# Gated projections interleaved with the last attention head, and cache value tiles taken in ordered pairs, in a two-layer decoder step

## The chip, the cores and the metric

The kernel runs on one core of a Trainium2 chip. The metric is the device time of one launch in microseconds (us). Five engines run their own instruction streams in order: TensorE (PE), VectorE (DVE), ScalarE (ACT), GpSimd (POOL) and SyncE (SP), which here issues the DMAs from one queue. Semaphores order them across engines.

## What is computed

One inference step of a two-layer trunk with width 1024, for 1024 prompt tokens and 64 decode tokens (8 sequences of 8), so T = 1088 columns. Layer 0 is a gated DeltaNet mixer. Layer 1, where the change lies, is a windowed attention with three head groups g of windows 128, 512 and 2048 (dilations 1, 4, 16), eight heads each, and a gate. Its core, cut:

```
proj = einsum('bld,de->ble', h, w_in)
qkv  = proj[..., :3*N_GROUPS*WIDTH_B].reshape(B, L, 3, N_GROUPS, H_B, DH_B)
z    = proj[..., 3*N_GROUPS*WIDTH_B:]
for gi, (window, dil) in enumerate(DIL_GROUPS):
    o, lse = dilated_attn_prompt(q, k, v, window, dil)     # prompt tokens
    o, lse = dilated_attn_step(q, k, v, kv_bufs[gi], ...)  # decode tokens, against the cache
wts = softmax(stack(lses, axis=0), axis=0)
o   = sum(wts[..., None] * stack(outs, axis=0), axis=0)
y   = einsum('ble,ed->bld', o.reshape(B, L, WIDTH_B) * silu(z), w_out)
```

Then follow a gated residual add and a final RMSNorm.

## The kernel before

**Products.** `project` (L122 to L135) makes 128 output columns for all T tokens: three chunks of 384, 384 and 320 tokens, each 8 slices of the contraction times 3 products (high and low parts of inputs and weights: `hh` with `whi`, `hl` with `whi`, `hh` with `wlo`), 72 PE instructions at L130. They accumulate in PSUM tiles `pp`, of which there are two.

**Layer 1's loop** runs over head pairs hp 0 to 3, in each over the groups g = 2, 1, 0, in each over the two heads a = 0, 1. For one (hp, g, a) there are three projections (`proj_tile`: v, k, q; copies at L1105, L1107, L1109), then `attention` with transposes of v and k (L1115), and eight blocks: scores L1151 on PE, mask and minimum L1154 on DVE, exponential L1156 on ACT, transposes L1160 on PE, a copy L1163 or L1165, and the product with the values L1169 on PE. Results go to `stg`; those of g = 2 and g = 1 are stored in DRAM (`gscr`).

**The combine.** After g = 0 of each head, `combine` (L1175 to L1206) weighs the three groups, twice, for four blocks of 128 tokens each ("half"): it loads the other groups' results `stgc` (L1181, two buffers), works out weights on DVE and ACT (L1187 to L1196), scales and adds (ACT L1200, DVE L72), transposes on PE (L1204, four), copies back into an `stgc` buffer (ACT L1205) and stores to `oscr` (L1206). The second half's loads go into the buffer from which the first half's store reads.

**Decode work** is pumped between projections from two queues of generators; `pump(x)` takes x units on average. `qk` holds `decode_scores`: cache key tiles `kc` (L1218, 512 KB), for g = 0 transposed on PE (L1262, four) and multiplied (L1270), for g = 1 and 2 multiplied on DVE with broadcast queries `qb` (L1303); the new tokens' rows at L1242, L1243, L1297, L1298. `pv` holds `decode_out`: per head pair 26 value tiles `vc` of 512 KB (loads L1225, four buffers), each multiplied by 8 small PE instructions at L1345 (two trace records each) into one accumulator; then L1354 sums and L1357 stores. A scheduler puts PE's instructions in one order; the value products of a tile are not tied together.

**After the last head.** The attention of hp 3, a 1, g 0 pumps 1.5 units of `pv` per block, with no projection beside it. Then the attention's pools are closed and new ones opened: eight z heads (`z_phase`, through `gate`: weights, loads `zo` of the attention's output from `oscr` at L397, 72 products, tanh, two DVE steps, and the split into `oh` and `ol`), with three `zo` and three `zt` buffers; then the output projection in two passes, and the normalised rows `yn` (PE L1434, ACT L1436, DVE L1438, store L1440) with three buffers.

## Time and profile before

| | |
|---|---|
| timed runs | 2485.02, 2466.92, 2469.04 us, median 2469.04 |
| profiled execution | 2477.78 us, its span 2476.1 us |
| PE busy | 2335.6 us, 94% |
| DVE busy | 1377.4 us, 56% |
| ACT busy | 926.0 us, 37% |
| POOL busy | 258.0 us, 10% |
| granted TensorE clock, mean over the span | 0.949 |
| read from and written to DRAM | 322.31 MB, 54.27 MB |

Times in the trace are us from the span's start. Layer 1's loop over the first three head pairs lies at about 1180 to 2200, the last head's combine and attention end at 2267.6, the z stage at 2362. A busy time is the sum of an engine's records; PE's records overlap a little, so the distance to the next record's start is the time that one takes up. The granted clock is a share of full speed: 1.0 is TensorE's level of 2.4 GHz, 0.5 that of 1.2 GHz, and values between are means over a stretch.

### The profile page before, as it was taken

To read this page: it belongs to the slowest core of one execution; us is meant where nothing else is said; L and a number is where in the kernel's file an instruction comes from. 1 tells how busy PE (TensorE), PEld (TensorE's weight loads), DVE (VectorE), ACT (ScalarE), POOL (GpSimd) and SP (SyncE) were. 2 spreads that over 40 slices of the span, in tenths; PEclk is the share of its full clock that TensorE was granted. 3 is DMA by queue.
4 is the path that set the end of the run, shared out by engine and by line. 5 is a ranking of instruction groups with operands and counts; after the bars stand their busy time and mean duration, and the time that the engine had idled before them with its cause. 6 is when DMAs were issued, how large, how long until landed. Compare 5 with 4: busy or idle time off the path is not lost.

```text
span 2476.1 us, 43143 instructions
## 1 busy us (share of the span) xinstructions
PE 2335.6 (94%) x16607; PEld 2168.3 (88%) x16607; DVE 1377.4 (56%) x3414; ACT 926.0 (37%) x2453; POOL 258.0 (10%) x399
## 2 busy tenths in 40 slices
PE   7789899989999999899999999999999999998998
PEld 5688788888888898899899999899998999985998
DVE  5678668767875537327743365533655336453434
ACT  5444444444453324233234332343323433232334
POOL 2222222222221202200000000000000000000000
PEclk9989899889899999799999999999999999988999
DMA  9232232232233256339832696626976269657334
GB/s 288 73 84 68 54 96 70 60 83 73 71 79 106 84 157 193 108 88 318 255 91 77 200 328 216 198 77 201 327 215 201 77 199 327 210 181 246 91 108 149
DMA packets 490575, 379.42 MB, mean 153 GB/s; under 512 B 46334, under 2 KB 465391, under 8 KB 490368
## 3 DMA queue, kind: packets, MB, share of 16 engines
q1 hardware_dynamic: 490368, 376.65, 51.6%
q8 instruction: 131, 2.15, 0.4%
q14 instruction: 76, 0.62, 0.1%
HBM read 322.31 MB, written 54.27 MB: 152 GB/s over the span
## 4 chain that ended last, share of the span: by engine, by line
PE 62%; DMA 14%; DVE 13%; issue 5%; ACT 3%; SPq 1%; POOL 1%; POOLq 0%; DVEq 0%; ACTq 0%
PE pp L130 42%; DMA qb<-qscr 3%; DMA DT<-gcscr 2%; PE ps L1151 2%; PE ps L1169 2%; PE sc L1345 2%; DVE ca L72 2%; DVE vtmp L686 2%; DMA wraw<-in_a_w_in_dram 1%; PE ps L1115 1%; DVE pr L1303 1%; DMA vc<-in_cache_kv_w_dram 1%; PE ps L1160 1%; PE ps L151 1%; DVE wlo L115 1%
## 5 line engine op out<-in xcount | busy, mean ns | idle before, releaser
L130 PE MATMUL pp<-hh,whi 128*128 128x384 f32 (+1 forms) x2688 | 913.1, 340 | 13.8 <-DVE cso L552 7.0
L130 PE MATMUL pp<-hl,whi 128*128 128x384 f32 (+1 forms) x2688 | 903.5, 336 | 1.1 <-POOL hl L212 1.1
L130 PE MATMUL pp<-hh,wlo 128*128 128x384 f32 (+1 forms) x2688 | 902.0, 336 | 0.7 <-DVE wlo L115 0.7
L130 PEld LDWEIGHTS pp<-hh,whi 128*128 128x128 f32 x2688 | 513.6, 191 | 31.2 <-issue 10.8
L130 PEld LDWEIGHTS pp<-hl,whi 128*128 128x128 f32 x2688 | 513.5, 191 | 9.2 <-issue 4.1
L130 PEld LDWEIGHTS pp<-hh,wlo 128*128 128x128 f32 x2688 | 511.7, 190 | 5.6 <-issue 2.1
L114 ACT CAST whi<-wraw 128x1024 fp32r<-128x1024 f32 x144 | 150.5, 1045 | 226.0 <-PE pp L130 150.7
L115 DVE TENSOR_TENSOR wlo<-wraw,whi 128x1024 fp32r<-128x1024 f32 x136 | 168.2, 1237 | 95.3 <-ACT whi L114 94.4
L1156 ACT ACTIVATE sm<-sm,stg 128x128 f32<-128x128 f32 (+1 forms) x192 | 86.6, 451 | 344.3 <-DVE stg L1154 312.5
L1303 DVE TENSOR_TENSOR pr<-kc,qb 128x1024 f32<-128x1024 f32 x128 | 154.7, 1218 | 78.9 <-DMA qb<-qscr 50.3
L1293 DVE TENSOR_REDUCE ST<-pr 128x8 f32<-128x1024 f32 x128 | 153.9, 1213 | 1.2
L417 POOL TENSOR_TENSOR ol<-zo,oh 128x384 fp32r<-128x384 f32 x7 | 7.1, 1020 | 1308.9 <-ACT oh L416 1308.9
L72 DVE SCALAR_TENSOR_TENSOR ca<-xin,cwT,ca 128x384 f32<-128x384 f32 (+1 forms) x216 | 133.7, 621 | 9.6 <-ACT ca L556 8.4
L1154 DVE CUSTOM_DVE_ANT_0 sm<-ps,mA 128x256 f32<-128x256 f32 (+1 forms) x128 | 48.4, 378 | 162.1 <-PE ps L1151 150.2
L1169 PE MATMUL ps<-vnat,pT 128*128 128x128 f32 x560 | 98.3, 283 | 5.4 <-DVE pT L1165 5.3
L686 DVE TENSOR_TENSOR vtmp<-Vi,Mi 128x2 f32<-128x2 f32 (+30 forms) x248 | 99.3, 400 | 4.7 <-PE lv L757 0.8
L1151 PE MATMUL ps<-kT,qT 128*128 128x128 f32 (+1 forms) x384 | 95.8, 332 | 5.1 <-DVE stg L1154 5.0
L1169 PEld LDWEIGHTS ps<-vnat,pT 128*128 128x128 f32 x560 | 85.5, 190 | 15.3 <-DVE pT L1165 8.1
L1345 PE MATMUL sc<-vc,Z 128*8 128x128 f32 x1664 | 80.9, 289 | 12.2 <-DMA vc<-in_cache_kv_w_dram 11.5
L1163 ACT COPY pT<-ps 128x256 f32<-128x256 f32 (+1 forms) x96 | 32.4, 338 | 132.7 <-PE ps L1160 129.0
L130 PE MATMUL pp<-oh,whi 128*128 128x384 f32 (+1 forms) x264 | 79.1, 330 | 0.8 <-DVE hh L72 0.8
L1345 PEld LDWEIGHTS sc<-vc,Z 128*8 128x8 f32 x1664 | 41.8, 91 | 39.8 <-DMA vc<-in_cache_kv_w_dram 18.2
(452 smaller groups left out, 3650.2 us busy)
## 6 DMA issues: line engine op xcount, KB each, us to landing
qb<-qscr SPq DMA_DIRECT2D x128, 512.0 KB
vc<-in_cache_kv_w_dram SPq DMA_DIRECT2D x104, 512.0 KB
kc<-in_cache_kv_w_dram SPq DMA_DIRECT2D x104, 512.0 KB
wraw<-in_b_w_in_dram SPq DMA_DIRECT2D x80, 512.0 KB
wraw<-in_a_w_in_dram SPq DMA_DIRECT2D x32, 512.0 KB
aw<-in_ada_w_dram SPq DMA_DIRECT2D x24, 512.0 KB
wraw<-in_ada_w_dram SPq DMA_DIRECT2D x24, 512.0 KB
stgc<-gscr SPq DMA_DIRECT2D x32, 260.0 KB
```

Of the source, the lines that this page charges most:

```text
L72: return (eng or V).scalar_tensor_tensor(out=out, in0=in0, scalar=scalar, in1=in1, op0=op0, op1=op1)
L114: A.copy(out=hi, in_=raw)
L115: (eng or V).tensor_tensor(out=lo, in0=raw, in1=hi.bitcast(F32), op=ALU.subtract)
L130: mm = PE.matmul(acc[:, :cn], lhsT=a[:, k, :], rhs=b[k][:, c0:c0 + cn], start=(n == 0), stop=(n == 3 * KD - 1))
L686: V.tensor_tensor(out=tv, in0=Vi[:, :na, :w], in1=Mi[:, :w, c].unsqueeze(1).broadcast_to([P, na, w]), op=ALU.mult)
L1151: PE.matmul(sv, lhsT=qT[:, b * P:(b + 1) * P], rhs=kT[:, k0:k0 + w], start=True, stop=True)
L1154: V.tensor_tensor_reduce(out=sm[:, :w], in0=sv, in1=mk, scale=1.0, scalar=3e38, op0=ALU.add, op1=ALU.min, accum_out=stg[:, b, 128:129])
L1156: A.activation(out=sm[:, :w], in_=sm[:, :w], func=AF.Exp, scale=-1.0, bias=stg[:, b, 128:129], accum_out=stg[:, b, 129:130])
L1169: PE.matmul(ob[:, (b % 4) * P:(b % 4 + 1) * P], lhsT=pT[:, i * P:(i + 1) * P], rhs=vnat[:, k0 // P + i, :], start=(i == 0), stop=(i == w / ...
L1293: V.tensor_reduce(out=sv[:, n:n + 4, :], in_=pr.rearrange("p (n a e) -> p n a e", a=2, e=P), op=ALU.add, axis=AX.X)
L1303: V.tensor_tensor(out=out, in0=k, in1=q, op=ALU.mult)
L1345: PE.matmul(od[32 * j:32 * j + 8, f * P:(f + 1) * P], lhsT=Z[g][:, a * NB + 2 * j + c, 8 * k:8 * k + 8], rhs=vc[:, j, a * P:(a + 1) * P], ...
```

## The change

Four things change in what runs, and the memory plan makes room for them.

1. `decode_scores` for g = 0 loads both key tiles first, then yields three units, and each key transpose is ordered behind the newest dense product (`newest[0]`).
2. `decode_out` takes value tiles in pairs: a pair is loaded one unit ahead, and all 16 instructions of two tiles are chained in one order, behind the newest product and at high priority. A unit is a pair, so the pumps are halved: 0.9 for 1.8, in the last head 0.5 for 1.5.
3. z head 0 begins after the fourth block of the last attention. The others follow, with 1.8 units of `pv` after each, and the rest of the values at head 6. `oh` and `ol` take slots of tiles that are done by then (`kc`, `qb`, `kT`, `qT`, `vT`, `vc`), which are widened to T columns; `zo` and `zt` are halves of one `KT` slot each: two buffers where there were three.
4. The final stage takes slots by tag too: `yn` has two buffers where it had three.

Tables of layer 0 (`cT`, `SH`, `SC`, `adr`) move into layer 0's pool. The number of PE matrix instructions is the same.

```diff
+    newest = [None]
 
     def project(w, hh, hl, cb, chunks=CHUNKS, each=None):
         whi, wlo = w
@@ -132,6 +130,7 @@
                     if each:
                         each(mm)
                     n += 1
+            newest[0] = mm
...
-        row = wp.tile([P, P], F32, name="adr", bufs=2)
+        row = lc.tile([P, P], F32, name="adr", bufs=2)
...
+    cT = lc.tile([P, KD, 32], F32, name="cT")
+    V.memset(cT, 0.0)
+    SHm = [lc.tile([P, KD, 9], F32, name=f"SH{l}") for l in range(2)]
+    SCm = [lc.tile([P, KD, 9], F32, name=f"SC{l}") for l in range(2)]
...
+    def wide(tag, bufs, name=None, dtype=F32):
+        t = sb.tile([P, T], dtype, name=name or tag, tag=tag, bufs=bufs)
+        return t if name else t[:, :1024]
     def load_cache(g, hp, i):
-        t = sb.tile([P, 4, 256], F32, name="kc", bufs=3)
+        t = wide("kc", 3).rearrange("p (q n) -> p q n", n=256)
...
-        new_rows(g, hp, kf, vf, vnew)
         ST = sb.tile([P, P], F32, name="ST", bufs=1)
         if g == 0:
+            kcs = [load_cache(g, hp, i) for i in range(NT[g])]
+            new_rows(g, hp, kf, vf, vnew)
+            for _ in range(3):
+                yield
             st = sbank()
             for i in range(NT[g]):
-                kc = load_cache(g, hp, i)
+                kc = kcs[i]
                 for a in range(2):
                     tb = sbank()
                     for q in range(4):
-                        PE.transpose(tb[:, q * P:(q + 1) * P], kc[:, q, a * P:(a + 1) * P], ident)
+                        t = PE.transpose(tb[:, q * P:(q + 1) * P], kc[:, q, a * P:(a + 1) * P], ident)
+                        order_after(t, newest[0], "the keys land behind the products before")
...
-                    qb = sb.tile([P, 1024], F32, name="qb", bufs=4)
+                    qb = wide("qb", 4)
...
-        for n, (g, c, k) in enumerate(tiles):
-            vc = load_values(g, hp, c, k)
-            for a in range(2):
-                f = c * 2 + a
-                for j in range(4):
-                    PE.matmul(od[32 * j:32 * j + 8, f * P:(f + 1) * P],
-                              lhsT=Z[g][:, a * NB + 2 * j + c, 8 * k:8 * k + 8], rhs=vc[:, j, a * P:(a + 1) * P],
-                              start=(n == 0 and a == 0), stop=(n == len(tiles) - 1 and a == 1))
+        def load(n0):
+            return [(t, load_values(t[0], hp, *t[1:])) for t in tiles[n0:n0 + 2]]
+        n, nxt = 0, load(0)
+        yield
+        for n0 in range(0, len(tiles), 2):
+            pair, nxt = nxt, load(n0 + 2)
+            prev = newest[0]
+            with tc.high_priority(offset=2000):
+                for (g, c, k), vc in reversed(pair):
+                    for a in range(2):
+                        f = c * 2 + a
+                        for j in range(4):
+                            mm = PE.matmul(od[32 * j:32 * j + 8, f * P:(f + 1) * P],
+                                           lhsT=Z[g][:, a * NB + 2 * j + c, 8 * k:8 * k + 8],
+                                           rhs=vc[:, j, a * P:(a + 1) * P],
+                                           start=(n < 4), stop=(n >= 8 * len(tiles) - 4))
+                            order_after(mm, prev, "one run of products for two value tiles")
+                            prev = mm
+                            n += 1
...
+    oh, ol = [], []
+    class Gated:
+        def __init__(self):
+            self.at = {n: [sb.tile([P, 1024], F32, name=n, tag="KT", bufs=2), 0] for n in ("zo", "zt")}
+        def tile(self, shape, dtype, name, tag, bufs):
+            e = self.at[name]
+            e[1] = 384 - e[1]
+            return e[0][:, e[1]:e[1] + 384]
+    gated = []
+    SLOTS = (("kc", 3), ("kc", 3), ("kc", 3), ("qb", 4), ("qb", 4), ("qb", 4), ("qb", 4), ("kT", 2), ("qT", 2), ("vT", 1),
+             ("kT", 2), ("qT", 2))
+    def z_head(h):
+        if not gated:
+            gated.append(Gated())
+        for i, o in enumerate((oh, ol)):
+            if h < 6:
+                o.append(wide(*SLOTS[2 * h + i], name=f"{'ol' if i else 'oh'}{h}", dtype=F32R))
+            else:
+                o.append(sd.tile([P, T], F32R, name=f"{'ol' if i else 'oh'}{h}", tag="vc", bufs=4))
+        z_phase(gated[0], W1_[:, 9216 + h * P:9216 + (h + 1) * P], h, hh, hl, oh, ol)
...
-                vT = sb.tile([P, NP], F32, name="vT", bufs=1)
-                kT = sb.tile([P, NP], F32, name="kT", bufs=2)
-                qT = sb.tile([P, NP], F32, name="qT", bufs=2)
+                vT = wide("vT", 1)
+                kT = wide("kT", 2)
+                qT = wide("qT", 2)
                 for part, d, ds in ((2, vT, vTs), (1, kT, kTs), (0, qT, qTs)):
                     proj_tile(g, part, h, d, ds)
                     qk.pump(2.2)
-                    pv.pump(1.8)
+                    pv.pump(0.9)
...
-                for _ in attention(g, h, qT, kT, vT, stg):
+                for n, _ in enumerate(attention(g, h, qT, kT, vT, stg)):
                     if last:
-                        pv.pump(1.5)
+                        pv.pump(0.5)
+                        if n == 3:
+                            z_head(0)
...
+    for h in range(1, NH):
+        if h == 6:
+            pv.pump(100.0)
+        z_head(h)
+        pv.pump(1.8)
+    class Last:
+        @staticmethod
+        def tile(shape, dtype, name, bufs):
+            full, tag = {"xr": ([P, 8, 130], "stg"), "sq": ([P, 8, P], "vnat"), "yn": ([P, 4, 130], "stgc")}[name]
+            t = sb.tile(full, dtype, name=name, tag=tag, bufs=2).rearrange("p a b -> p (a b)")
+            return t[:, :shape[1]]
...
+                yn = mp.tile([P, 512], F32, name="yn", bufs=2)
...
     l1.close()
-    zp = ExitStack()
-    zpool = zp.enter_context(tc.tile_pool(name="zp", bufs=1, reuse_waits="tile"))
-    oh, ol = ([zpool.tile([P, T], F32R, name=n, bufs=6) for _ in range(6)] for n in ("oh", "ol"))
-    with tc.tile_pool(name="zt", bufs=1, reuse_waits="tile") as zt:
-        for h in range(NH):
-            if h == 6:
-                pv.pump(100.0)
-                for o in (oh, ol):
-                    o += [sd.tile([P, T], F32R, name=f"oh{i}", tag="vc", bufs=4) for i in range(2)]
-            z_phase(zt, W1_[:, 9216 + h * P:9216 + (h + 1) * P], h, hh, hl, oh, ol)
-            pv.pump(4.0)
...
-                    yn = mp.tile([P, 512], F32, name="yn", bufs=3)
```

The scheduler's order shows what moves on PE. First, PE between the two halves of the combine of the second head pair's first head, before: the last rows ahead of the second half's transpose (line 1204), with the new tokens' rows, two key tiles' transposes from `kc` and their products with `KT`.

```order
L1297 MATMUL lv<-ident,ST 128x128
L1298 MATMUL lv<-kTs,qTs 128x128
L1242 MATMUL lv<-ident,kTs 128x128
L1243 MATMUL lv<-ident,vTs 128x128
L1262 MATMUL lv<-ident,kc 128x128 x4
L1270 MATMUL lv<-qTs,KT 128x8 x4
L1262 MATMUL lv<-ident,kc 128x128 x4
L1204 MATMUL ps<-ident,stg 128x128
```

The same place after, whole, from the first half's four transposes (now line 1207) to the second half's:

```order
L1207 MATMUL ps<-ident,stg 128x128 x4
L128 MATMUL pp<-hh_11264,wlo 128x384
L1310 MATMUL lv<-ident,ST 128x128
L1311 MATMUL lv<-kTs,qTs 128x128
L1250 MATMUL lv<-ident,kTs 128x128
L1251 MATMUL lv<-ident,vTs 128x128
L1172 MATMUL ps<-vnat,pT 128x128 x2
L1207 MATMUL ps<-ident,stg 128x128
```

The key tiles' rows are gone from this place, and of the 20 products that stood ahead of them before only one is left between the two halves.

Second, PE in an attention of the last head pair, before: value tiles (`vc`) between an attention's rows and the products of a projection.

```order
L130 MATMUL pp<-hh_11467,wlo 128x320
L1345 MATMUL sc<-vc,Z_11559 8x128 x8
L1345 MATMUL sc<-vc,Z_11560 8x128
L1169 MATMUL ps<-vnat,pT 128x128
L1151 MATMUL ps<-kT,qT 128x128
L1345 MATMUL sc<-vc,Z_11560 8x128
L1160 MATMUL ps<-ident,sm 128x128
L1345 MATMUL sc<-vc,Z_11560 8x128 x6
L130 MATMUL pp<-hh_10928,whi 128x384
```

After, a value row in such a place (the line is now 1365, a product 128):

```order
L128 MATMUL pp<-hh_11467,wlo 128x320
L1365 MATMUL sc<-vc,Z_11561 8x128 x16
L1163 MATMUL ps<-ident,sm 128x128
L1154 MATMUL ps<-kT,qT 128x256
L128 MATMUL pp<-hh_10928,whi 128x384
```

Before, one tile's eight instructions stand in pieces with attention rows between; after, two tiles' sixteen stand in one row.

Third, PE at the end of the last attention, before: the rows from the last head's first half to the first z products.

```order
L1204 MATMUL ps<-ident,stg 128x128 x4
L1345 MATMUL sc<-vc,Z_11560 8x128 x8
L1169 MATMUL ps<-vnat,pT 128x128 x2
L1345 MATMUL sc<-vc,Z_11560 8x128 x8
L1345 MATMUL sc<-vc,Z_11561 8x128 x72
L1204 MATMUL ps<-ident,stg 128x128 x2
L1345 MATMUL sc<-vc,Z_11561 8x128 x8
L1204 MATMUL ps<-ident,stg 128x128 x2
L1345 MATMUL sc<-vc,Z_11561 8x128 x32
L130 MATMUL pp<-hh_11286,whi 128x320
L130 MATMUL pp<-hl_11287,whi 128x320
```

After, from the third of the last four transposes to the value pairs behind them:

```order
L1207 MATMUL ps<-ident,stg 128x128
L128 MATMUL pp<-hl_11417,whi 128x320
L128 MATMUL pp<-hh_11416,wlo 128x320
L128 MATMUL pp<-hh_11441,whi 128x320
L128 MATMUL pp<-hl_11442,whi 128x320
L128 MATMUL pp<-hh_11441,wlo 128x320
L1207 MATMUL ps<-ident,stg 128x128
L128 MATMUL pp<-hh_11467,whi 128x320
L128 MATMUL pp<-hl_11468,whi 128x320
L128 MATMUL pp<-hh_11467,wlo 128x320
L1365 MATMUL sc<-vc,Z_11560 8x128 x32
L128 MATMUL pp<-hh_10928,whi 128x384
```

Before, no product stands beside the last values, and the z products begin behind them; after, z products stand between the transposes of the last half, and two value pairs behind them (the others stand among later z products).

## Rows read from the trace of the kernel before

**Rows 1.** The page: busy us, share and instructions of each engine; costliest groups, lines left out.

```profile
PE 2335.6 (94%) x16607; PEld 2168.3 (88%) x16607; DVE 1377.4 (56%) x3414; ACT 926.0 (37%) x2453; POOL 258.0 (10%) x399
...
L1345 PE MATMUL sc<-vc,Z 128*8 128x128 f32 x1664 | 80.9, 289 | 12.2 <-DMA vc<-in_cache_kv_w_dram 11.5
```

**Rows 2.** Windows: start:end us, busy PE, PEld, DVE, ACT, POOL (records), clock, DMA share, GB/s.

```profile
2205.90:2226.00 20.10, 17.92 (x80) 16.23 (x79) 7.83 (x36) 8.60 (x25) 0.00 (x0) 0.58 0.21 53
2226.00:2240.70 14.70, 13.31 (x199) 9.82 (x199) 7.30 (x38) 7.62 (x27) 0.00 (x0) 1.00 0.78 243
2240.70:2267.60 26.90, 15.84 (x252) 7.20 (x248) 4.67 (x21) 3.55 (x10) 0.00 (x0) 0.66 1.06 340
2267.60:2362.00 94.40, 94.40 (x595) 93.02 (x592) 41.73 (x71) 31.90 (x58) 8.16 (x8) 0.99 0.31 88
```

**Rows 3.** Timeline, PE, tail: start us, busy us, engine, line, operation, count [idle before <-releaser].

```profile
2228.18 1.06 PE L1345 MATMUL sc<-vc,Z 128*8 128x128 f32 x32
2229.17 0.49 PE L1333 MATMUL lv<-pTn,vnew 128*128 128x128 f32 x2
...
2266.64 1.04 PE L1345 MATMUL sc<-vc,Z 128*8 128x128 f32 x16 [2.29 <-DMA vc<-in_cache_kv_w_dram]
2267.62 0.64 PE L130 MATMUL pp<-hh,whi 128*128 128x320 f32 x1
```

**Rows 4.** Timeline, PE, one value tile in an attention of the second head pair.

```profile
1570.50 0.39 PE L1345 MATMUL sc<-vc,Z 128*8 128x128 f32 x4
1570.83 0.71 PE L1169 MATMUL ps<-vnat,pT 128*128 128x128 f32 x4
1571.47 0.40 PE L1345 MATMUL sc<-vc,Z 128*8 128x128 f32 x6
...
1573.12 0.38 PE L1345 MATMUL sc<-vc,Z 128*8 128x128 f32 x2
1573.43 0.44 PE L130 MATMUL pp<-hh,whi 128*128 128x384 f32 x1
1573.71 0.34 PE L130 MATMUL pp<-hl,whi 128*128 128x384 f32 x1
```

**Rows 5.** Timeline, all engines, combine of the second head pair's first head.

```profile
1579.23 0.60 PE L1204 MATMUL ps<-ident,stg 128*128 128x128 f32 x4
...
1579.67 0.75 PE L1354 MATMUL lv<-comb,odS 128*128 128x32 f32 x6
...
1580.48 0.37 SPq L1206 DMA_DIRECT2D oscr<-stgc  x1
...
1582.85 0.37 SPq L1181 DMA_DIRECT2D stgc<-gscr  x1
...
1585.76 0.17 DVE L1187 TENSOR_TENSOR cm<-cm,stgc 128x4 f32<-128x4 f32 x1 [5.01 <-DMA stgc<-gscr]
...
1590.03 0.33 PE L1204 MATMUL ps<-ident,stg 128*128 128x128 f32 x1 [0.31 <-DVE stg L72]
...
1590.20 1.78 PE L1115 MATMUL ps<-ident,vT 128*128 128x128 f32 x8
...
1592.01 0.81 DVE L1109 COPY vT<-pp 128x384 f32<-128x384 f32 x1 [0.72 <-PE ps L1115]
```

**Rows 6.** Windows at the second head pair's two combines, columns as in rows 2.

```profile
1579.20:1597.40 18.20, 15.36 (x92) 14.64 (x91) 7.50 (x29) 5.70 (x14) 0.00 (x0) 0.81 0.35 98
1635.20:1648.70 13.50, 11.23 (x74) 10.93 (x72) 5.07 (x22) 4.99 (x13) 0.00 (x0) 0.87 0.28 85
```

**Rows 7.** Timeline, all engines, the end of the program.

```profile
2470.62 0.69 ACT L1436 ACTIVATE yn<-ps,rn 128x512 f32<-128x512 f32 x1 [2.15 <-DMA out_y_p_dram<-yn]
```

**Rows 8.** Groups by line, PE, 1180 to 2200: busy us, mean ns, idle before, releasers.

```profile
L1345 PE MATMUL sc<-vc,Z 128*8 128x128 f32 x1248 | 59.9, 273 | 0.0
...
L1270 PE MATMUL lv<-qTs,KT 128*128 128x8 f32 x96 | 13.6, 267 | 6.7 <-ACT KT L1265 4.1 <-DVE cm L1194 1.7 <-ACT stg L1200 0.9
...
L1262 PE MATMUL lv<-ident,kc 128*128 128x128 f32 x48 | 8.9, 308 | 4.9 <-DVE nmd L1299 4.9
```

More of the change, by code (lines that the diff above doesn't have):

```diff
@@ L94 @@
     fgv = vecs[:, 65:73]
-    cT = const.tile([P, KD, 32], F32, name="cT")
-    V.memset(cT, 0.0)
     fold = const.tile([P, 9], F32, name="fold")
@@ L100 @@
         V.tensor_tensor(out=fold, in0=fold, in1=ident[:, i:i + 9], op=ALU.add)
-    SHm = [const.tile([P, KD, 9], F32, name=f"SH{l}") for l in range(2)]
-    SCm = [const.tile([P, KD, 9], F32, name=f"SC{l}") for l in range(2)]
     GTm = [const.tile([P, KD, 9], F32, name=f"GT{l}") for l in range(2)]
@@ L1273, in decode_scores @@
         else:
+            new_rows(g, hp, kf, vf, vnew)
             tb = sbank()
@@ L1441 @@
-    zp.close()
+    for h in range(1, NH):
[9 more added lines that the diff above has]
+            return t[:, :shape[1]]
+    x2 = [Columns("hh", F32) for _ in range(KD)]
@@ new lines, with post2 @@
+    mp = Last
+    for chunks, c0, c1 in ((PASSES[0], 0, WIDE // P), (PASSES[1], WIDE // P, NC + 1)):
+        cs = slice(chunks[0][0], sum(chunks[-1]))
+        def post2(j):
+            A.activation(out=x2[j][:, cs], in_=x2[j][:, cs], func=AF.Copy, scale=fgv[:, j:j + 1])
+        qs = out_project(mp, 1, I["b_w_out"][0], x1scr, x2, oh, ol, post2, chunks)
+        rn = col_stats(qs, c0, c1)
+        for c in range(c0, c1):
+            m = rows(c)
+            for half in range(2):
+                yn = mp.tile([P, 512], F32, name="yn", bufs=2)
+                tb = bank()
+                for q in range(4):
+                    PE.transpose(tb[:m, q * P:(q + 1) * P], x2[half * 4 + q][:, tok(c)], ident)
+                if half:
+                    A.activation(out=yn[:m], in_=tb[:m, :], func=AF.Copy, scale=rn[:m, c:c + 1])
+                else:
+                    V.tensor_scalar(out=yn[:m], in0=tb[:m, :], scalar1=rn[:m, c:c + 1], scalar2=None, op0=ALU.mult)
+                dst = O["y_p"][0, tok(c), :] if c < NC else O["y_s"].rearrange("b l d -> (b l) d")
+                SY.dma_start(out=dst[:, half * 512:(half + 1) * 512], in_=yn[:m])
```

20 lines of the change are left out of this document (removed).

## The prediction

> **What bounds the kernel now.** I read the page's busy shares first: TensorE (PE) is busy for 94% of the span [rows 1], so only time in which PE is idle, slowed or issuing inefficiently can be won. Next the windows by stage, which set PE's busy time beside the granted clock. The z stage is dense at 0.99 [rows 2]; the 61.7 us ahead of it, 2205.9 to 2267.6, are not: 17.92 busy of 20.1 at a clock of 0.58, 13.31 of 14.7 at 1.00, 15.84 of 26.9 at 0.66 [rows 2]. This is the tail, with the last head's combine, its attention and the 26 value tiles of the last head pair, and no dense product to put beside them. In its last third DMA is full (1.06, 340 GB/s) and PE waits for value tiles, 11.5 us in the whole run by the page's group [rows 1]; the last tile comes after 2.29 us of idling, and the z products start right behind it [rows 3]. Third, PE's rows inside attention, where one value tile is cut in pieces [rows 4]. Fourth, all engines at a combine, a chain over five queues [rows 5].
>
> The profiled execution took 2477.78 us (span 2476.1), 0.35% over the median of 2469.04. I work the difference out of the profile and take it off the median.
>
> **1. Tail: gain 17 (6 to 28).** How much of the 61.7 us is content? Upper bound: busy time times clock, 17.92x0.58 + 13.31 + 15.84x0.66 = 34.2. Lower: 26 tiles at 0.495 (two tiles took 0.99, from 2228.18 to the next row at 2229.17 [rows 3]) make 12.9; the windows hold 80 + 199 + 252 records, less 26x16 for the tiles leaves 115, by no less than 0.11 (four L1204 take 0.44 to the next row [rows 5]): 12.7, together 25.6. So content is 26 to 34 and the loss 28 to 36; I take the middle, 32. In the new order z products stand between the attention's blocks and value pairs among later z products, so the loss can be filled. I leave 15:
> - 6.5 for the combine of the last pair's first head, which stays ahead of any z product: its chain needs 12.8 us (part 3), the order puts 6.9 beside it, and the clock falls behind the gap as it does now.
> - 4.5 (0 to 7) for value pairs. A pair is 1.05 MB, 3.1 us at 340 GB/s [rows 2], and I add 2.9 for landing, as a 260 KB load takes from issue to reader [rows 5]: 6.0. Four buffers hold two pairs; where the pump takes two in a row, the order has some 35 products between them, 5.6 us at the z stage's 0.16 a record (595 in 94.4 us [rows 2]). I let 0.5 us stick out at each of the last nine pairs.
> - 3 for the end of z: the last value tile's sums (L1354) and the output stores now stand some 41 products (7 us) ahead of the output projection, and zo has two halves where it had three buffers.
> - 1 for switches.
> The bounds are the loss's lower end with 22 left (pairs waiting throughout), 6, and 36 less 8, 28.
>
> On the pairs' loads the Trainium skill says otherwise ("DMA: Bandwidth & Descriptors", section on the anatomy of one DMA): about 2.0 us fixed plus bytes over 436 GB/s; by this a pair would land in 4.4 us, an estimate, the 4.5 above would be nothing and the tail's gain 21.5. The trace reached 340 GB/s here. Nothing below uses the page's figure.
>
> **2. Whole value tiles: gain 10 (5 to 15).** Before, one tile stands in four pieces of 4, 6, 4 and 2 records (the second of 4 is not shown), 0.38 to 0.40 busy each and 0.31 to 0.33 to the next row (1570.50 to 1570.83, 1573.12 to 1573.43) [rows 4]: 1.3 us against 0.495 whole. Over the first three head pairs the line is busy for 59.9 us in 1248 records [rows 8]; 39 whole pairs would be 39x1.06 = 41.3. A record's end overlaps the next by 0.06 a run, and the order has 32 runs a head pair before, 13 after: 59.9 - 96x0.07 = 53.2 elapsed against 39x0.99 = 38.6, so 15 is saved. But the products themselves are cut into 395 runs where there were 368; a switch costs about 0.19 (the first product behind another line is busy for 0.44 where the next is for 0.34 [rows 4], and the first instruction behind the products holds about as much more): -5. Fifteen if the switches hide, five if the pairs find their loads late.
>
> **3. Combine at the six g = 0 transitions of the first three head pairs: loss 8 (16 lost to 2 gained).** Both halves share buffers, so the second runs behind the first: the L1204 transposes at 1579.23, the store at 1580.48, the load's issue at 1582.85 (2.4 later), the first reader at 1585.76 (2.9 later), the second half's L1204 at 1590.03, 10.8 us after the first. Behind it, and behind eight value transposes (1.78), the copy L1109 at 1592.01 frees the bank that the next projection needs: 12.8 us from the L1204 [rows 5]. PE's time without content is 12.8 less the work that stands between. Before, the order puts 7.0 to 7.8 there at all six: 5.4 each, 32 in all; the windows of two of them lose 18.2 - 15.36x0.81 = 5.8 and 13.5 - 11.23x0.87 = 3.7 [rows 6], so 32 is on the high side by up to 4. After, the cache keys are moved away and I count, row by row at such prices, between the two L1207: 7.5, 3.7, 1.4, 9.9, 1.4, 9.9 (the order of the second head pair shows a 1.4). Where the wait is short (three places) the eight value transposes can stand in it, 1.8 less, and with 0.2 to 0.7 for the half clock behind the long ones: 3.5 + 9.3 + 12.1 + 1.1 + 12.1 + 1.1 = 39. So -8. Not worse than -16: that doubles it. Up to +2: before, PE also waited at these places for the new rows' maximum and the key copies, 4.9 + 6.7 = 11.6 us [rows 8]; if it was these that set the pace, they disappear, since the key transposes now lie among products, and pay for most of the longer gap.
>
> **4. Output buffers: loss 3 (0 to 5).** The normalised rows have two buffers where they had three. At the end a copy already waits 2.15 us for an output store [rows 7]; with two buffers the last six pieces wait once more, +2, and the first pass about once, +1. Nothing if the reciprocal before them is later than the buffers.
>
> **5. The rest: 0 (3 either way).** Tables in the first layer's pool and wider slots change no instruction. The first four value loads move behind other loads on SP's queue at the layers' boundary; those are spaced by their own two buffers.
>
> **Sum**: 17 + 10 - 8 - 3 = 16: 2461.8 for the profiled execution, 2453 against the median.
>
> **The rivals.**
> - *Bare combines cost nothing and the loads are in time (faster).* Part 3 at +2, 8 left in the tail (gain 24), and 10 - 3: 33, 2436. For it: PE's named releasers at the transitions are maxima and key copies, not the combine alone [rows 8]. Against: the chain in [rows 5] is fixed and longer than what the new order puts beside it.
> - *Value pairs starve the z stage (slower).* SP issues pair loads, z's weights and the zo loads from one queue; a pair's load waits there for its buffers, and a zo load behind it is late, or the other way round, and PE stands at a pair because the order places it. Price: a fully exposed pair is 6.0 us; eight in the z stage are 48, less the 4.5 counted: 16 - 43.5 = -27.5, 2496. It decides when the mean wait per pair passes (16 + 4.5)/8 = 2.6 us. For it: DMA at 1.06 in the tail and a pair wait of 2.29 for one tile. Against: z leaves 0.69 of DMA free [rows 2], and two units lie on average between a load and its products.
> - *The filling doesn't happen.* PE runs in order, so where a block of the last attention is late, the z products behind it are late too: tail gain 0, the rest 10 - 8 - 3 = -1, 2470. Against: the z products stand in front of the late instructions in most places of the new order.
>
> **How the numbers follow.** My forecast 0.47 (own range 2441 to 2465), fast rival 0.33 (2425 to 2445), starved z 0.10 (2475 to 2500), no filling 0.10 (2465 to 2475). A measurement of this kernel can tell about 1% from no change, 2444.3 and 2493.7. Faster: nine tenths of the fast rival and a fifth of mine, 0.39. Slower: half of the starved case and a little for a layout cost that I don't see, 0.08. Same 0.53. The range reaches from the fast rival's far end, 2425, to 2480, and leaves out most of the starved case and some of parts 2 and 3 at their ends together.
>
> **What would show it.** Right: PE dense at clock 0.95 or more from the last attention to the output projection, with the stretch from 2205.9 to the z stage's end some 17 shorter; the value line's busy time over the first three pairs falling from 59.9 to about 41; and gaps of 9 to 12 us with a clock under 0.8 at the first-head combines of the second and third head pair. Wrong: value waits of over 2.6 us per pair in z, a low clock in the last attention, or short gaps at those combines.

## The result and the profile after

The changed kernel took 2448.71 us in the median of four runs (2437.65 to 2461.96) against 2475.33 (2466.92 to 2485.02): a ratio of 0.9887, with a 95% interval of 0.9848 to 0.9926. A second timing gave 0.9903 (0.9874 to 0.9933). The prediction was 2453, with a range of 2425 to 2480. The medians of the kernel before lie between 2469 and 2486 from one session to the next, so below a run is compared by its ratio to the before of its own session, or with runs of the same session.

Its profiled execution has a span of 2446.5 us, 29.6 less than before, at a mean clock of 0.951 (0.949 before). The page, engines and the first groups of products; the columns are those of rows 1:

```profile
PE 2294.7 (94%) x16607; PEld 2164.4 (88%) x16607; DVE 1378.7 (56%) x3414; ACT 929.2 (38%) x2453; POOL 256.7 (10%) x399
```

PE has 41 us less busy time [rows 1] with as many instructions; the other engines are as they were.

To find where the time went, I take the start of the same dense product in both traces, counting PE's rows that write `pp` from `hh`, `hl`, `oh` or `ol`. The second timing left a second trace of the changed kernel, which stands beside the first:

| product | what stands there | before | after | second trace after | after - before, both traces |
|---|---|---|---|---|---|
| no. 2376 | end of layer 0 | 978.2 | 977.2 | 976.9 | -1.0, -1.3 |
| no. 7344 | last one ahead of the last head's projections | 2141.8 | 2132.3 | 2138.7 | -9.5, -3.1 |
| no. 7560 | last of that head's projections | 2190.8 | 2177.9 | 2184.4 | -12.9, -6.4 |
| no. 8208 | early in the output projection | 2371.4 | 2339.6 | 2346.7 | -31.8, -24.7 |
| no. 8712 | its end | 2461.9 | 2430.6 | 2437.6 | -31.3, -24.3 |
| | end of the span | 2476.1 | 2446.5 | 2453.5 | -29.6, -22.6 |

The stretch from no. 7344 to no. 8208, the last head and z, is 22 us shorter in both traces; 3.4 of it fall in the head's projections, 18 to 19 behind them. The loop ahead of it gains 8.5 us in the first trace and 1.8 in the second, so its share is known only to some 7 us. Behind no. 8208 about 2 us are given back. The windows of the tail, which answer to [rows 2], with the same columns:

```profile
2191.90:2205.90 14.00, 11.21 (x75) 10.57 (x74) 5.43 (x23) 5.95 (x15) 0.00 (x0) 0.80 0.32 100
2205.90:2226.00 20.10, 20.10 (x154) 19.50 (x154) 11.46 (x43) 11.82 (x31) 1.06 (x1) 0.97 0.65 184
2226.00:2245.20 19.20, 19.20 (x154) 18.42 (x153) 10.07 (x31) 9.66 (x30) 1.53 (x2) 1.00 0.42 127
2245.20:2262.00 16.80, 16.80 (x164) 16.17 (x165) 8.61 (x28) 6.58 (x16) 0.47 (x1) 1.00 0.73 223
2262.00:2340.00 78.00, 73.93 (x690) 70.49 (x684) 27.09 (x44) 22.14 (x39) 5.07 (x5) 0.98 0.60 187
```

From 2205.9 to 2262 PE is dense at a clock of 0.97 to 1.00, where it had gaps in all three windows and a clock of 0.58, 1.00 and 0.66 [rows 2]. What is left is the last pair's first combine (14.0 - 11.21x0.80 = 5.0) and 4 us of idling up to the output projection. PE's waits from 1180 on (sum, times, longest) name that idling, one wait for values and one ahead of the output projection:

```profile
PE pp L128 <- DVE zt L72: 2.7, 1, 2.7
...
PE sc L1365 <- DMA vc<-in_cache_kv_w_dram: 1.4, 1, 1.4
```

The groups by line on PE from 1180 to 2190, which answer to [rows 8]; columns as there. The first line is the combine's transposes before, from 1180 to 2200, the others are after:

```profile
L1204 PE MATMUL ps<-ident,stg 128*128 128x128 f32 x50 | 11.5, 332 | 3.8 <-DVE stg L72 3.8
...
L1365 PE MATMUL sc<-vc,Z 128*8 128x128 f32 x1216 | 40.1, 273 | 0.0
...
L1282 PE MATMUL lv<-qTs,KT 128*128 128x8 f32 x96 | 11.7, 242 | 0.0
L1207 PE MATMUL ps<-ident,stg 128*128 128x128 f32 x48 | 10.9, 338 | 31.6 <-DVE stg L72 29.3 <-ACT knew L1253 2.3
L1273 PE MATMUL lv<-ident,kc 128*128 128x128 f32 x52 | 8.5, 277 | 0.0
```

The value line is busy for 40.1 us in 1216 records (59.9 in 1248 before), the key rows wait for nothing (11.6 before), and the combine's transposes, L1207, now have 31.6 us of idling ahead of them, where L1204 had 3.8. That is the new wait. All engines but PE's products at the second pair's first combine, to hold against [rows 5]:

```profile
1575.55 0.17 DVE L1189 TENSOR_TENSOR cm<-stg,stgc 128x4 f32<-128x4 f32 x1 [0.67 <-DMA stgc<-gscr]
...
1578.91 0.60 PE L1207 MATMUL ps<-ident,stg 128*128 128x128 f32 x4
...
1579.55 0.59 ACT L1208 COPY stgc<-ps 128x512 f32<-128x512 f32 x1
...
1580.16 0.37 SPq L1209 DMA_DIRECT2D oscr<-stgc  x1
...
1582.70 0.37 SPq L1184 DMA_DIRECT2D stgc<-gscr  x1
...
1585.63 0.17 DVE L1190 TENSOR_TENSOR cm<-cm,stgc 128x4 f32<-128x4 f32 x1 [5.13 <-DMA stgc<-gscr]
...
1589.06 0.45 PE L1207 MATMUL ps<-ident,stg 128*128 128x128 f32 x1 [8.37 <-DVE stg L72]
```

The second half starts on its first load at 1575.55, ahead of the first half's transposes; what it waits for is its second load, which is issued only at 1582.70, behind the store of 1580.16 from that same buffer. That it is the store's landing, and not other work in SP's queue, that releases such loads shows in SP's waits from 1180 to 2200 (sum, times, longest); this one ends at 1582.64:

```profile
SPq L1184 <- DMA oscr<-stgc: 16.7, 9, 4.1
```

PE stands for 8.37 us in one piece.

### The profile page after: what moved, and what is told of

Its sections match the earlier page's. It is cut to its first block, busy times and chain, and to the rows that moved or that the text cites. A ratio compares the mean times of both kernels' runs of the same rounds, so it can differ in the third digit from the quotient of the medians.

```text
span 2446.5 us, 43164 instructions
## 1 busy us (share of the span) xinstructions
PE 2294.7 (94%) x16607; PEld 2164.4 (88%) x16607; DVE 1378.7 (56%) x3414; ACT 929.2 (38%) x2453; POOL 256.7 (10%) x399
## 4 chain that ended last, share of the span: by engine, by line
PE 67%; DMA 13%; DVE 10%; issue 6%; ACT 2%; POOL 1%; SPq 1%; POOLq 0%; ACTq 0%; DVEq 0%
PE pp L128 46%; DMA DT<-gcscr 2%; PE ps L1154 2%; PE ps L1172 2%; DMA qb<-qscr 2%; PE sc L1365 2%; PE ps L1118 1%; DMA aw<-in_ada_w_dram 1%; DVE ca L72 1%; DVE vtmp L689 1%; DMA wraw<-in_a_w_in_dram 1%; PE ps L1163 1%; DVE pr L1316 1%; DMA out_kv_s_dram<-knew 1%; PE ps L150 1%
## 5 line engine op out<-in xcount | busy, mean ns | idle before, releaser
L72 DVE SCALAR_TENSOR_TENSOR ca<-xin,cwT,ca 128x384 f32<-128x384 f32 (+1 forms) x216 | 137.3, 638 | 9.6 <-ACT ca L559 8.4
L72 DVE SCALAR_TENSOR_TENSOR hh<-pp,GT,xr 128x384 f32<-128x384 f32 (+1 forms) x48 | 27.3, 571 | 85.0 <-PE pp L128 83.6
L128 PE MATMUL pp<-oh,whi 128*128 128x384 f32 (+1 forms) x216 | 72.0, 333 | 2.7 <-DVE zt L72 2.7
L1157 DVE CUSTOM_DVE_ANT_0 sm<-ps,mG 128x128 f32<-128x128 f32 x64 | 18.4, 288 | 96.5 <-PE ps L1154 67.1
```

What stands on the lines that cost most here:

```text
L72: return (eng or V).scalar_tensor_tensor(out=out, in0=in0, scalar=scalar, in1=in1, op0=op0, op1=op1)
L128: mm = PE.matmul(acc[:, :cn], lhsT=a[:, k, :], rhs=b[k][:, c0:c0 + cn], start=(n == 0), stop=(n == 3 * KD - 1))
L1157: V.tensor_tensor_reduce(out=sm[:, :w], in0=sv, in1=mk, scale=1.0, scalar=3e38, op0=ALU.add, op1=ALU.min, accum_out=stg[:, b, 128:129])
```

## The experiments

Ratios are to the kernel before in the same session.

| run | edit, on which kernel | ratio | 95% interval |
|---|---|---|---|
| changed kernel, first, again | | 0.9887, 0.9903 | 0.9848 to 0.9926, 0.9874 to 0.9933 |
| e1_z_behind | changed: z head 0 written behind the attention | 0.9889 | 0.9868 to 0.9909 |
| e1b_z_held | and its products held behind the last combine | 0.9969 | 0.9950 to 0.9987 |
| e2_tiles_single | changed: value tiles single | 0.9918 | 0.9897 to 0.9938 |
| e3_keys_early | changed: keys where they were before | 0.9857 | 0.9836 to 0.9878 |
| e4_late_half | changed: second half of combine later | 0.9815 | 0.9785 to 0.9845 |
| e5_store_stg | changed: the half stored from another tile | 0.9734 | 0.9706 to 0.9763 |
| e6_both | e4 and e5 | 0.9694 | 0.9667 to 0.9721 |
| e7_before_store | before, with e5's edit alone | 0.9846 | 0.9820 to 0.9872 |
| e8_both_keys | e6 with the keys where they were before | 0.9760 | 0.9736 to 0.9784 |
| e9_both_yn3 | e6 with a third output buffer | 0.9714 | 0.9692 to 0.9737 |

**z behind, and z held.** First only the place in the code is undone:

```diff
-                        if n == 3:
-                            z_head(0)
-    for h in range(1, NH):
+    for h in range(NH):
```

> The changed kernel (ratio to before 0.9887, span 2446.5) with z head 0 written behind the last attention instead of behind its fourth block; slots, value pairs and everything else as in the changed kernel. Theory A (where the z head is written makes the z products available): the last attention has no product beside it again, and 20 to 30 us come back: ratio 0.996 to 1.001. Theory B (what keeps z back in the kernel before is that its tiles need the space of the closed attention pools; with slots by tag the scheduler takes z products forward on its own): no change, ratio 0.985 to 0.992, and z products between the last combine's halves as in the changed kernel.

It made no difference: 0.9889. The scheduler takes z products forward by itself, and 74 of them still stand between the last combine's halves in its order; the same stretch is dense here too:

```profile
2195.00:2262.00 67.00, 63.98 (x569) 61.28 (x570) 31.54 (x104) 31.42 (x82) 3.11 (x3) 0.95 0.60 177
```

So the place in the code is not what makes z products available, and theory A falls. Theory B's other half, that in the kernel before z is kept back by the closed pools, is supported by that kernel's own trace, which shows more than the section on the change says: 48 of the 72 products of z head 0 run there from 2194.0 on, ahead of the last attention. They fill the two `pp` tiles, and the copies out of these into `zt`, a tile of the new pools, come only behind the last transposes. Before, then after:

```profile
2194.00 0.44 PE L130 MATMUL pp<-hh,whi 128*128 128x384 f32 x1
...
2261.20 0.88 ACT L408 ACTIVATE zt<-pp 128x384 f32<-128x384 f32 x2
```

```profile
2203.84 0.88 ACT L411 ACTIVATE zt<-pp 128x384 f32<-128x384 f32 x2
```

No run puts the pools back under the changed kernel, so the slots are the likeliest cause and not a tested one. Then the products themselves are held back:

```diff
+            lastT[0] = PE.transpose(tb[...], X[0][:, n, 0:P], ident)      # in combine
-        z_phase(gated[0], W1_[...], h, hh, hl, oh, ol)
+        gate(gated[0], W1_[...], h, hh, hl, z_split(h, oh, ol),
+             each=(lambda mm: order_after(mm, lastT[0], "...")) if h == 0 else None)
```

> As e1_z_behind, and z head 0's products are ordered behind the last transposes of the last combine, so that no z product stands in the last attention; 26 value tiles still in pairs, most of them among z products. Theory A (the tail's 22 us in the profile come from z products beside the last attention): 15 to 30 us over the changed kernel, ratio 0.994 to 1.000, with clock about 0.6 and idle PE between the last head's transposes. Rival C (they come from value tiles that no longer wait at the end, since their loads spread over the z stage): at most 8 us over the changed kernel, ratio up to 0.992.

It fell to 0.9969, about 20 us over the changed kernel. From product 7344 to 8208 its trace takes 230.9 us, the changed kernel's 207.3, that of before 229.6. Its windows over the last attention show PE with gaps and at a low clock, as before:

```profile
2196.00:2206.00 10.00, 7.72 (x87) 5.72 (x85) 3.40 (x14) 2.02 (x7) 0.00 (x0) 0.71 0.95 288
2206.00:2226.00 20.00, 15.75 (x91) 13.59 (x87) 7.42 (x36) 11.42 (x33) 0.00 (x0) 0.72 0.55 157
2226.00:2262.00 36.00, 24.30 (x118) 20.29 (x119) 12.80 (x60) 12.06 (x35) 0.00 (x0) 0.81 0.24 67
```

All value pairs of the last head pair lie among z products here, and it helps nothing: rival C falls. (In the changed kernel three pairs of 13 still stand in the attention, so the run moves those too.) The changed kernel's gain in the tail is that of products beside the attention.

**Single value tiles.** The code of before for the values, with pumps of 1.8, 1.0 and 3.6:

```diff
-            pair, nxt = nxt, load(n0 + 2)      # and the chained order at high priority
+            vc = load_values(g, hp, c, k)      # one tile, eight products, no order
-                    pv.pump(0.9)
+                    pv.pump(1.8)
```

> The changed kernel with value tiles one at a time, not tied together, loaded in their own unit, and the pumps doubled (1.8, 1.0 and 3.6); all else as changed. The order then has 117 runs of value rows for 47. Theory A (whole tiles gain 10 to 19 us: 15 from the rows' prices over the first three pairs and up to 4 in the last): 8 to 20 us over the changed kernel, ratio 0.991 to 0.997, the value line's busy time over the first three head pairs back near 60 from 41. Rival D (the pairs' pace is what leaves the combines bare, and the shorter rows are given back there): in this order 6.6 and 4.4 us stand in the second and third head pair's combines for 1.0 and 9.1, so the bare gaps shorten by 6 to 8 us and the net is 0 to 8 us over the changed kernel, ratio 0.987 to 0.991.

The ratio of 0.9918 is 0.15 to 0.31 points over the changed kernel's two, 4 to 8 us, between the two theories. The intervals overlap; but e1_z_behind, which times like the changed kernel, took 2453.5 to 2458.7 us in the same session and this kernel 2460.1 to 2472.4, so the sign stands. Its lines on PE tell why (1180 to 2200):

```profile
L1358 PE MATMUL sc<-vc,Z 128*8 128x128 f32 x1168 | 56.6, 273 | 0.0
L1207 PE MATMUL ps<-ident,stg 128*128 128x128 f32 x48 | 11.7, 348 | 18.3 <-DVE stg L72 15.8 <-ACT knew L1253 2.4
...
L1367 PE MATMUL lv<-comb,odS 128*128 128x32 f32 x16 | 3.8, 404 | 8.4 <-ACT odS L1363 8.4
```

The value rows cost about what they did before (56.6 busy in 1168 records), and the combines' transposes wait for 18.3 us in place of 31.6. Not all of the difference is gained: the 8.4 us ahead of the value sums (L1367), which are new, stand in the same combines, 4.2 each at 1597.8 and 1908.6. From the first half's transposes to the second half's, PE idles for 26.6 us over the six combines ahead of the last pair, for 31.7 in the changed kernel. So the pairs' pace lays the combines bare by some 5 us, whole tiles gain more than that, and both theories are half right.

**Keys early.**

```diff
-            kcs = [load_cache(g, hp, i) for i in range(NT[g])]
-            for _ in range(3):
-                yield
-                        order_after(t, newest[0], "...")
+                kc = load_cache(g, hp, i)
```

> The changed kernel with the g = 0 key tiles loaded, transposed and multiplied as in the kernel before (no three units of delay, no order behind products). Theory A (the moved keys took the cover from the combines): the six gaps shrink by 8 to 12 us in sum and the time falls by that, ratio 0.984 to 0.986. Rival D (it is not the keys but the pairs' pace; the order still has 1.1 us in the first combines of the second and third head pair): only the first pair's second combine gains (8.6 for 3.2 us, about 5 us), and waits of the keys' own (some 10 us of maximum and key copy in the kernel before) come back: ratio 0.987 to 0.993.

0.9857, some 7 to 11 us better than the changed kernel by the ratios, with intervals that overlap; against e1_z_behind in the same session (2453.5 to 2458.7) every one of its times, 2442.9 to 2453.0, is lower. The idling ahead of the transposes falls to 17.6 us and little of the key waits returns (1.9 + 1.2 + 1.3):

```profile
L1278 PE MATMUL lv<-qTs,KT 128*128 128x8 f32 x96 | 12.2, 251 | 3.2 <-DVE KT L1275 1.9 <-ACT KT L1273 1.2
...
L1207 PE MATMUL ps<-ident,stg 128*128 128x128 f32 x48 | 10.3, 315 | 17.6 <-DVE stg L72 17.0 <-ACT knew L1253 0.5
L1270 PE MATMUL lv<-ident,kc 128*128 128x128 f32 x52 | 8.3, 279 | 1.3 <-DVE nmd L1307 1.3
```

So the moved keys uncover part of the combines as well. Between the halves of the six combines PE idles for 21.8 us here: of the 31.7, the keys' old place takes away 10, single tiles 5, and neither covers them.

**The combine itself.** The next two attack the round trip from two sides: put it beside products, or shorten it. Later:

```diff
-                    for half in range(2):
-                        combine(h, stg, half)
+                    if hp == 3:
+                        combine(h, stg, 0); combine(h, stg, 1)
+                    else:   # due counts heads; taken behind the k projection of that head
+                        if a:
+                            late.append((6 * hp + 6, h, stg, 0, False))
+                        else:
+                            combine(h, stg, 0)
+                        late.append((6 * hp + 6 + a, h, stg, 1, True))   # True: ordered behind newest[0]
```

> The changed kernel with the second half of the six combines of the first three head pairs written two projections later, its transposes ordered behind the products written before it (35 to 45 us of work now stand between the halves' transposes for 1.0 to 9.1); loads, buffers and arithmetic as they were. Theory A (the combine's round trip lies bare in the changed kernel and costs what PE waits there, 29.3 us before the second transposes, with the low clock behind some 40): 25 to 40 us under the changed kernel, ratio 0.972 to 0.979, and the wait of the transposes on the weighted sum gone. Rival E (PE would wait in these places anyway, for the copies of the projections that free its banks, 6.4 us now, and for the next attention): 0 to 10 us under, ratio 0.985 to 0.989, with the banks' wait grown to 15 us or more.

0.9815, 18 to 22 us under the changed kernel, less than theory A asked. The edit also writes the first half of a pair's second head later. From the first half's transposes to the second half's, the trace has 38 to 48 us in the first three pairs, nearly all of it work; yet 12.7 us of the wait remain (PE's waits from 1180, longest last):

```profile
PE ps L1207 <- DVE stg L72: 12.7, 3, 5.8
PE pp L128 <- DVE vT L1112: 6.8, 4, 2.3
```

They are at 1338.5, 1641.3 and 1940.1, at the first half of the pair's second head: the delayed second half of one head is now followed closely by the first half of the next, and those two share the buffers. The wait moved to the neighbour in the buffers' ring. Rival E isn't right either: the banks' wait stays at 6.8.

The other side needs two lines:

```diff
-        A.copy(out=X[1][:, :, 0:P], in_=v3(tb))
-        SY.dma_start(out=oscr[h]..., in_=X[1][:, :, 0:P])
+        A.copy(out=X[0][:, :, 0:P], in_=v3(tb))
+        SY.dma_start(out=oscr[h]..., in_=X[0][:, :, 0:P])
```

> The changed kernel, but the transposed half goes back into the attention's own result tile and is stored from there, so that the second half's loads need not wait for the store: the round trip of 9.9 us from the first transposes to the second loses the copy, the store and its landing, 3.5 to 3.9 us; nothing is reordered. Theory A (the round trip is what PE waits for): the five bare gaps of 2.3 to 8.5 us shrink by up to 3.7 each, 12 to 18 us under the changed kernel, ratio 0.981 to 0.984. Rival E: 0 to 6 us, ratio 0.986 to 0.989.

0.9734: 38 to 42 us under the changed kernel by the ratios (the two medians of its session differ by 40), more than twice what I expected. All engines but the products, second pair's first combine, in this kernel:

```profile
1569.65 0.37 SPq L1184 DMA_DIRECT2D stgc<-gscr  x1
...
1574.58 0.17 DVE L1190 TENSOR_TENSOR cm<-cm,stgc 128x4 f32<-128x4 f32 x1 [0.59 <-DMA stgc<-gscr]
...
1577.03 0.60 PE L1207 MATMUL ps<-ident,stg 128*128 128x128 f32 x4
...
1578.28 0.36 SPq L1209 DMA_DIRECT2D oscr<-stg  x1
...
1580.95 0.30 PE L1207 MATMUL ps<-ident,stg 128*128 128x128 f32 x1 [2.15 <-DVE stg L72]
```

From the first transposes to the second it takes 3.9 us instead of 10.15. My estimate took away the copy, the store and its landing only. But once the store doesn't hold the buffer, the load is issued at 1569.65, seven microseconds ahead of the first half's transposes, so the load and the second half's weights leave the chain too; what remains is the scaling L72 behind the last block of attention. DVE also no longer stands for 5 us at L1190 with the next blocks' work behind it. Over the six combines ahead of the last pair the times from the first transposes to the second fall from 67.5 to 41.9 us in sum. In the traces, 26.4 us are gained from product 2376 to 7344 and 3.2 more up to 8208, 29.6 against the first trace of the changed kernel; against the second, in which this stretch is 7.4 us longer, it is 37.0. The timing's 38 to 42 lies a little above the second; single executions of one kernel differ by as much.

> e4_late_half and e5_store_stg together. Theory A: once the halves are apart, the shorter round trip is hidden in the first three pairs and only the last pair's first combine gains: ratio 0 to 0.002 below e4_late_half's. Rival E: as e4_late_half. If the two add fully (12 us below e4 or more), the cover of e4 isn't where the time went.

0.9694: 2407.66 us where the changed kernel took 2458.63 and before 2483.67 in that session. That is 29.5 us under e4_late_half's 2437.16, so theory A and rival E both fail and the third case holds: what e4_late_half put beside the combines was not where most of the time went. Against e5_store_stg's 2418.65 the later halves add 11 us. The transposes' idling is gone:

```profile
L1207 PE MATMUL ps<-ident,stg 128*128 128x128 f32 x56 | 8.6, 273 | 0.0
```

From product 2376 to 7344 it is 37.4 us shorter than the changed kernel's first trace and 44.1 shorter than its second; I take that as what the combines cost there.

**The same two lines in the kernel before.**

> The kernel before with e5_store_stg's edit alone (the half is stored from the attention's result tile, so the second half's loads don't wait for the store). Theory A (in the kernel before, too, the round trip outlasts the 7.0 to 7.8 us of work beside it, about 32 us over six combines; the edit takes some 6 us off each trip, as it did in the changed kernel, 10.1 to 3.9 in the second pair's first combine): 15 to 30 us under before, ratio 0.988 to 0.994. Rival F (before, PE's waits there are those for the new rows' maximum and the key copies, which stay): 0 to 8 us under, ratio 0.997 to 1.000.

0.9846, 38 us, more than either theory, and more than the whole change under study gained. From product 2376 to 7344 it gains 20.7 us, the round trips that the prediction had put at 32; from 7344 to 8208 another 18.6, in the tail, which I had not thought of. From 7560 to 8208 it takes 161.1 us, as the changed kernel does (161.7, before 180.6), and with no z product beside the last attention: 48 stand ahead of it, as in the kernel before, and the next one starts at 2229.9, behind it. So products beside the attention are one way to the tail's gain and not the only one; in the kernel before, the combines' stores held the attention up as well. The windows of the second pair's combines, against [rows 6]:

```profile
1584.20:1594.00 9.80, 9.75 (x71) 9.49 (x70) 6.80 (x26) 4.95 (x13) 0.00 (x0) 1.00 0.55 156
1633.80:1645.00 11.20, 11.20 (x87) 11.13 (x86) 4.75 (x12) 4.99 (x11) 0.00 (x0) 1.00 0.21 46
```

Dense at full clock, with the keys where they were. Of PE's 11.6 us of waits for maxima and key copies [rows 8] 0.5 are left, in the tail. That fits engines DVE and ACT that stood at the combine's load with this work behind them in their queues; it is read from the waits, not tried by itself. Rival F falls.

**Keys and output buffers, on e6.**

> e6_both with the g = 0 keys loaded, transposed and multiplied as in the kernel before. Theory A (the keys' move pays where it doesn't uncover the combine: the waits for the maximum and the key copies, 11.6 us in the kernel before, are what it removes): with the combines covered the old place costs 4 to 12 us, ratio 0.971 to 0.974. Rival G (the keys' place is indifferent by itself): ratio 0.968 to 0.971 as e6_both (0.9694).

0.9760 against 0.9694 and 0.9714 of kernels with the moved keys: 0.5 to 0.7 points, 11 to 16 us, over the upper end of theory A; rival G falls. By the medians of its own session it is 9.4 us over e9_both_yn3, of which some 2 belong to that kernel's third output buffer, and from product 2376 to 7344 the traces have 6 to 8 us (1124.0 against 1117.7 in e6_both and 1116.4 in e9_both_yn3). So the direction stands and the size is some 6 to 16 us. With the combines bare, in e3_keys_early, the sign is the other one.

> e6_both with a third buffer for the normalised output rows, taken from the slot of the natural keys. Theory A (two buffers cost 2 to 3 us at the end): the last 20 us of the trace are 2 us shorter; ratio 0.968 to 0.969, which the timing can't tell from e6_both's 0.9694; the trace decides.

0.9714, and in the same session as e8. The time can't tell it from e6. In the traces the last six pieces of the output run from 2398.85 to 2405.28 in e6, with four waits for a store's landing, and from 2396.70 to 2400.96 here, with two: 2.2 us less. The last piece in each:

```profile
2405.28 0.68 ACT L1504 ACTIVATE yn<-ps,rn 64x512 f32<-64x512 f32 x1 [2.19 <-DMA out_y_p_dram<-yn]
```

```profile
2400.96 0.68 ACT L1511 ACTIVATE yn<-ps,rn 64x512 f32<-64x512 f32 x1 [0.74 <-DMA out_y_p_dram<-yn]
```

## Why the prediction came out right, and where it didn't

The sign and the range came out as forecast. The size is less clear a hit than 2449 against 2453 looks, because the median of before had moved by 6 us in between: by the ratios, 0.9887 and 0.9903 of the 2469.04 that the prediction started from are 2441 to 2445, the lower end of my own range and the upper end of the fast rival's. 24 to 27 us of gain lie between my forecast's 16 and the rival's 33. What tells the two apart is the mechanism: the rival needed bare combines that cost nothing, and PE idles for 31.6 us at them. The terms:

1. **Tail, 17 (6 to 28): 18 to 19**, from no. 7560 on, in both traces; the last head's projections, which the term left out, give 3.4 more. That the products do it is shown by e1b_z_held: without them that stretch takes 185.9 us (before 180.6, changed kernel 161.7). By e7_before_store it is not the only way. What is left was less than I had set aside in two places: 5.0 at the combine instead of 6.5, and one wait of 1.4 for values instead of 4.5. At the end of z there are 2.69 us of idling and 3.4 us at a granted clock of 0.5 behind them. The step on the pairs' loads had 5.6 us between a load and its products; in the trace the last nine pairs have 6.3 to 23 us from the second tile's load to the first product. By the fit that the Trainium skill gives ("DMA: Bandwidth & Descriptors", the anatomy of one DMA) this part would have been nothing; that section gives it for loads issued by way of GpSimd, and these go through SP. The one pair that PE waited for, issued at 2291.3 and 2291.8 behind another pair, was read at 2299.45, 7.7 us behind the second issue, which is longer than the fit's 4.4 and than my 6.0; no row shows how long a pair's transfer takes by itself.
2. **Whole tiles, 10 (5 to 15): more, some 16.** The value line's busy time fell as worked out (41 forecast; 40.1 in 1216 of 1248 records). Measured to the next row, a tile takes 0.50 us where it took 0.68 on average before: 14 us over 78 tiles, for the 15 worked out. The 5 us against it, for more runs of products, were too many: to the next row, the 4968 products from no. 2376 to 7344 take 870.2 us for 868.0 (871.9 in the second trace). And a term was missing: the attention's rows, no longer cut by value rows, take 148.7 us there for 154.7 (155.5 with single tiles, in e2_tiles_single).
3. **Combines, -8 (-16 to 2): worse, at or past the lower bound.** The count from the order was right: less PE's idling, the times from the first half's transposes to the second half's are 7.9, 4.0, 1.8, 10.2, 1.8 and 10.2 us, for 7.5, 3.7, 1.4, 9.9, 1.4 and 9.9. The gaps at the first heads of the second and third pair are 8.4 and 8.6 us long, at clocks of 0.77 and 0.69, for the 9 to 12 that were to show it. The step that failed is the price of a gap, 12.8 us less the work, because it counts to the copy that frees the bank: PE's idling ends at the second half's transposes, which stand 9.9 to 10.9 us behind the first ones at all six places before. So PE idles there for 2.3 to 2.9 us each before, 15 in all and not 32, and for 32 after, where the sum had 39. With the low clock and the other waits that go with them, the combines cost, as an estimate, 37 to 44 us after (what e6_both gains on that stretch) and 21 before (what e7_before_store gains): a loss of 16 to 23. The reason given, "the cache keys are moved away", was part of it, since single tiles cover some of the idling too. The upper bound of +2 failed as well: I held it possible that the maxima and key copies set the pace before, and in e7_before_store those waits go with the round trip.
4. **Output buffers, -3 (0 to -5): -2.2** from no. 8208 on, and 2.2 by e9_both_yn3.

Parts 2 and 3 made 2 together and measured 8.5 in one trace, 1.8 in the other. That they met is partly luck: the rows gained more than I said, the combines lost more, and the two errors have opposite signs.

The starving rival needed 2.6 us per pair; the trace has 1.4 in all. That nothing is filled is excluded by the windows of the tail.

What the prediction didn't see is the larger matter. The prediction laid out the chain over the store in [rows 5] and took it as fixed. Each link had its row: the store at 1580.48, the next load's issue at 1582.85. The load waited for a buffer that a store was reading, and naming the holder of the buffer would have shown that another tile could carry the store. That was worth 38 us alone, before the change, and 38 to 42 after it.

## What to carry to other kernels

Where a chain runs from a store to a load of the same buffer, ask what holds the buffer before asking what could be put beside the wait: two lines here gained more than a rebuilt schedule. By the ratios the two gains add up (0.9846 and 0.9887 alone, 0.9734 together); in the tail they overlap (19 and 22 us alone, 25 together), and in the loop, where the rebuilt schedule had laid the round trips bare, they do more than add. Count from the order what stands beside a fixed round trip, at each place, whenever work is moved: moving it for its own waits can lay another chain bare. And before crediting the line that starts a stage earlier, undo that line alone; here it made no difference.

## What the runs showed of the hardware that was not expected

A 256 KB store held its source for 2.5 us before the next load into it was issued (1580.16 to 1582.70) and for 2.3 to 4.5 us at the nine places from 1180 to 2200 where SP waited for it; a load's reader came 2.9 us behind the issue, as before the change. Behind the 2.69 us of idling ahead of the output projection, the granted clock is 1.0 for the first microsecond and then 0.5, the level of 1.2 GHz, from 2326.6 to 2330.0. Rows of 384 columns stand 0.32 us apart there, where the same rows stand 0.17 apart at 1.0:

```profile
2325.55 0.44 PE L128 MATMUL pp<-oh,whi 128*128 128x384 f32 x1 [2.69 <-DVE zt L72]
...
2327.14 0.52 PE L128 MATMUL pp<-ol,whi 128*128 128x384 f32 x1
2327.46 0.52 PE L128 MATMUL pp<-oh,wlo 128*128 128x384 f32 x1
```

So a bare chain costs more than its idling: the first combines of the second and third pair have 6.68 and 6.65 us of busy time in 15.1 and 15.2, at a granted clock of 0.77 and 0.69.

```profile
1578.90:1594.00 15.10, 6.68 (x40) 6.11 (x39) 5.98 (x26) 5.28 (x14) 0.00 (x0) 0.77 0.29 78
1883.80:1899.00 15.20, 6.65 (x37) 6.07 (x35) 5.68 (x24) 5.23 (x13) 0.00 (x0) 0.69 0.30 77
```
